# Sixteen wide matmuls, then sixteen narrow ones, and four buffers instead of three for the split weights

## The chip, the cores and the metric

The kernel runs on one core of a Trainium2 chip. Its time is the device time in microseconds (us) of one execution; the number that counts is the median of the runs. Five engines work side by side, each through its own list of instructions in order: TensorE (PE, with its weight loads PEld), VectorE (DVE), ScalarE (ACT), GpSimd (POOL, idle here) and SyncE (SP, which issues the DMAs).

## The reference

One decoder layer on a sequence of 256 tokens with 2048 features, in float32:

```python
h = rmsnorm(x, norm1_g) * (1 + sc1) + sh1              # sh, sc, g: columns of silu(c) @ w_ada
q_sb, k_sb, v_sb, q_ds, k_ds, v_ds, q_ix, k_ix, w_ix = split(h @ w_in)
o_sb = stick_breaking_attention(q_sb, k_sb, v_sb)       # 8 heads of 128
o_ds = dsa_attention(q_ds, k_ds, v_ds, q_ix, k_ix, w_ix)
x = x + g1 * (concat(rmsnorm(o_sb), rmsnorm(o_ds)) @ w_out)
h2 = rmsnorm(x, norm2_g) * (1 + sc2) + sh2
u = causal_conv3(h2 @ w_up);  gate, val = split(u)      # 2 x 5504 columns
x = x + g2 * ((silu(gate) * val) @ w_down)
return rmsnorm(x, final_norm_g)
```

## The kernel before

**Arithmetic.** The large products take float32 operands in two parts: a high part rounded to the matmul's 32-bit format and a low part that holds the rest. Each product is three products: high by high, high by low and low by high. `load` brings 1 MB of weights (128 x 2048) into one of four buffers called raw; a `wa` load, with the weights of the modulation vector, shares these four. `split` cuts a load into two halves of 1024 columns: ACT casts a half into a high tile `wh` (L145), and DVE subtracts it to get the low tile `wl` (L146). High and low tiles each rotate through three buffers, so ACT can cast a half only when PE has finished with the half three before it.

**Stages.** The program goes through the input projections (A, B, V, QK), the sparse attention, the eight stick-breaking heads, the output projection O, and the FFN (U is w_up, W is w_down). Up to the first eight column tiles of U, `trn` or `nat` issue three matmuls for each block of 128 features: in `trn`, L166 (high by high), L167 (high weights by the low part of the activations) and L168 (low weights), each with 256 columns. From the ninth column tile of U on, and in all of W, `fold` treats a half load of eight blocks: eight matmuls of 512 columns, in which the high weights meet the high and the low activations side by side (L160), then eight of 256 columns with the low weights (L162). There are 70 such loads in U and 43 in W, 113 in all, each with 32 matmuls.

**Heads.** One head (`sb_head`) is a chain between engines: three lines of PE make z (L664 to L666); ACT goes over it four times (L668 to L672); DVE ends the softplus (L673); PE makes u from it (L675, L676); DVE adds (L678), ACT takes exp (L679), PE makes o (L681, L682); ACT scales and squares it (L683, L688), and DVE adds the squares up (L689). Weights of the QK and O stages lie between these lines on all engines. In the same stretch PE makes four columns of the modulation vector (L195), which ACT copies to `rw` (L200) and PE transposes into `aq` (L203).

**Norms.** The rows of squares go through `rms_b`: PE sums them (`rsbp`, L115), ACT takes ln and exp (L119, L123), DVE sharpens the result in four small steps (L121 to L126), PE spreads it over the partitions (`rsbb`, L129) and ACT copies it out (L132). For the heads, `norm_o` then multiplies the heads by it (L647), ACT casts them to `osh` (L649) and DVE subtracts to get `osl` (L650). The second half of the rows of `w_out` (tiles `wO`m`1`) is multiplied with these two; the first half (`wO`m`0`) meets `odh` and `odl`, which come from the sparse attention earlier. The norm ahead of the FFN has the same form (`r2p`, `r2b`), followed by L305 to L307, which make the FFN's input.

**Order.** The Python text doesn't fix the order of work between independent steps. The framework's scheduler lays out each engine's list when the program is built; it takes the readiness of operands and the free buffers as it models them and otherwise keeps the order of the text. On the chip an engine follows its list as it stands.

Of the kernel before, what the change touches and what calls it, by code (L numbers as in the profile page):

```python
# [11 lines left out]
F32R = mybir.dt.float32r  # L12
BF16 = mybir.dt.bfloat16
I32 = mybir.dt.int32
AF = mybir.ActivationFunctionType
ALU = mybir.AluOpType
# [3 lines left out]
P = 128  # L20
# [18 lines left out]
PB, PN1, PN2, PSG, PDG, PCW, PCB, PC, PGF = 0, 96, 112, 128, 136, 144, 402, 488, 504  # L39
# [15 lines left out]
def layer(ctx: ExitStack, tc: tile.TileContext, a, out):  # L55
    nc = tc.nc
    V, A, T, DMA = nc.vector, nc.scalar, nc.tensor, nc.sync

    cp = ctx.enter_context(tc.tile_pool(name="cp", bufs=1))
    wp = ctx.enter_context(tc.tile_pool(name="wp", bufs=1))  # L60

    def b8(shape, dt, name):
        return wp.tile(shape, dt, name=name, tag="b8", bufs=17)

    def s2(shape, dt, name):
        return wp.tile(shape, dt, name=name, tag="s2", bufs=3)
# [6 lines left out]
    def ps(name, dt=F32, tag="ps"):  # L73
        pool, bufs = psum_pool[0]
        return pool.tile([P, 512], dt, name=name, tag=tag, bufs=bufs[tag])


    par = cp.tile([P, PW], F32, name="par")
# [23 lines left out]
    mod = cp.tile([P, 96], F32, name="mod")  # L102
# [3 lines left out]
    def rb(name):  # L106
        return wp.tile([P, S], F32, name=name, tag="rb", bufs=2)
# [27 lines left out]
    def load(src, n, name):  # L135
        w = wp.tile([P, 2048], F32, name=name, tag="raw", bufs=4)
        DMA.dma_start(out=w[:, 0:n], in_=src)
        return w
# [1 line left out]
    lo_ = [None, None]  # L140

    def split(w, off, n, name):
        wh = wp.tile([P, 1024], F32R, name=name + "h", tag="wh", bufs=3)
        wl = wp.tile([P, 1024], F32R, name=name + "l", tag="wl", bufs=3)
        lo_[1] = A.copy(out=wh[:, 0:n], in_=w[:, off:off + n])  # L145
        lo_[0] = V.tensor_tensor(out=wl[:, 0:n], in0=w[:, off:off + n], in1=wh[:, 0:n].bitcast(F32), op=ALU.subtract)  # L146
        return wh, wl

    def nat(pt, xh, xl, wh, wl, first, last):
# [2 lines left out]
        T.matmul(pt, lhsT=xh, rhs=wl, start=False, stop=False)  # L152
        T.matmul(pt, lhsT=xl, rhs=wh, start=False, stop=last)

    def fold(steps):

        for pt, x, wh, _, first, _ in steps:
            T.matmul(pt, lhsT=wh, rhs=x, start=first, stop=False)  # L160
        for pt, x, _, wl, _, last in steps:
            T.matmul(pt[:, 1, :], lhsT=wl, rhs=x[:, 0, :], start=False, stop=last)  # L162

    def trn(pt, xh, xl, wh, wl, first, last):

        T.matmul(pt, lhsT=wh, rhs=xh, start=first, stop=False)  # L166
        T.matmul(pt, lhsT=wh, rhs=xl, start=False, stop=False)  # L167
        T.matmul(pt, lhsT=wl, rhs=xh, start=False, stop=last)  # L168
# [14 lines left out]
    for i in range(1, 4):  # L183
        V.tensor_tensor(out=sq1[0][:, 0:4, :], in0=sq1[0][:, 0:4, :],
                        in1=sq1[i // 2][:, (i % 2) * 4:(i % 2) * 4 + 4, :], op=ALU.add)
# [25 lines left out]
    def order(later, earlier):  # L211
        tc.add_manual_dep(later.ins, earlier.ins.name,
                          mybir.DependencyInfo(mybir.DependencyClass.NoSync, mybir.DependencyReason.DATA),
                          reason="order")
# [57 lines left out]
    for g in range(4):  # L272
        pt = ps(f"cb{g}")
        for j in range(4):
            k = 4 * g + j
# [7 lines left out]
                           op1=ALU.mult)  # L283
    b1 = cp.tile([P, KT], F32, name="b1")
    V.scalar_tensor_tensor(out=b1, in0=par[:, PB + 16:PB + 32], scalar=1.0, in1=par[:, PN1:PN1 + KT], op0=ALU.add,
                           op1=ALU.mult)
# [228 lines left out]
    pt = ps("kixp", tag="att")  # L515
# [8 lines left out]
    for t in range(NT):  # L524
        for g in range(2):
            pt = ps(f"qixp{t}{g}", tag="att")
# [12 lines left out]
    for t in range(NT):  # L539
# [4 lines left out]
        for g in range(8 // npb):  # L544
            pts = [ps(f"rel{t}{g}{par_}", tag="att") for par_ in range(2)]
            for j in range(npb):
                for par_ in range(2):
                    T.matmul(pts[par_][:, j * L:(j + 1) * L],  # L548
                             lhsT=qixT[par_ * ID:(par_ + 1) * ID, g * npb + j, t * P:(t + 1) * P],
                             rhs=kixT[par_ * ID:(par_ + 1) * ID, 0:L], start=True, stop=True)  # L550
            for par_ in range(2):
                rl = s2([P, npb, L], F32, f"rl{t}{g}{par_}")
                A.activation(rl, pts[par_].rearrange("p (n l) -> p n l", n=npb), AF.Relu)  # L553
                for j in range(npb):
                    h = (g * npb + j) * 2 + par_
                    if sacc[par_] is None:
                        sacc[par_] = sc_t(L, f"sacc{t}{par_}")
                        if par_ == 0:
                            V.scalar_tensor_tensor(out=sacc[0], in0=rl[:, j, :], scalar=wix[:, t, h:h + 1], in1=cmt,
                                                   op0=ALU.mult, op1=ALU.add)  # L560
                        else:
                            V.tensor_scalar(out=sacc[1], in0=rl[:, j, :], scalar1=wix[:, t, h:h + 1], scalar2=None,
                                            op0=ALU.mult)
                    else:
                        V.scalar_tensor_tensor(out=sacc[par_], in0=rl[:, j, :], scalar=wix[:, t, h:h + 1],  # L565
                                               in1=sacc[par_], op0=ALU.mult, op1=ALU.add)
# [15 lines left out]
    pt = ps("kdsp", tag="att")  # L582
# [4 lines left out]
    for t in range(NT):  # L587
        for g in range(2):
            pt = ps(f"qdsp{t}{g}", tag="att")
# [6 lines left out]
    for t in range(NT):  # L596
# [4 lines left out]
        for g in range(NH // npb):  # L601
            pt = ps(f"lg{t}{g}", tag="att")
            pv = pt.rearrange("p (n l) -> p n l", n=npb)
            T.matmul(pv, lhsT=identb, rhs=mb[t].rearrange("p (n l) -> p n l", n=1).to_broadcast([P, npb, L]),
                     start=True, stop=False)
            for j in range(npb):
                T.matmul(pv[:, j, :], lhsT=qdsT[:, g * npb + j, t * P:(t + 1) * P], rhs=kdsT[:, 0:L],
                         start=False, stop=j == npb - 1)
# [8 lines left out]
            for j in range(npb):  # L617
                h = g * npb + j
                A.activation(pr[:, h, :], pr[:, h, :], AF.Copy, scale=rec[:, j:j + 1])
        for s_ in range(t + 1):  # L620
            for g in range(2):
                pt = ps(f"pp{t}{s_}{g}", tag="att")
# [3 lines left out]
        for g in range(2):  # L626
            pt = ps(f"av{t}{g}", tag="att")
            pv = pt.rearrange("p (k t) -> p k t", k=4)
            for s_ in range(t + 1):
                T.matmul(pv, lhsT=a2[:, s_, 80 + HD:80 + 2 * HD], rhs=pT[:, s_, 4 * g:4 * g + 4, :],  # L630
                         start=s_ == 0, stop=s_ == t)
            A.activation(dsq[:, 4 * g:4 * g + 4, t * P:(t + 1) * P], pv, AF.Square)
            for j in range(4):
                h = 4 * g + j
# [76 lines left out]
    acc = [ps(f"O{m}", tag="acc") for m in range(4)]  # L711
# [11 lines left out]
    resid_i, last = [None, None], [None, None]  # L723
    x1T = [b8([P, 8, S], F32, f"x1T{i}") for i in range(2)]
    sq2 = ws[:, 1536:1792]

    def resid(dst, acc, gate, res, sqsum, k, name):

        resid_i[0] = V.scalar_tensor_tensor(out=dst, in0=acc, scalar=gate, in1=res, op0=ALU.mult, op1=ALU.add)  # L729
        if k == 0:  # L730
            A.activation(sqsum, dst, AF.Square)
            return None
        sq = s2([P, S], F32, f"{name}{k}")
        resid_i[1] = A.activation(sq, dst, AF.Square)  # L734
        if k >= KT - 2:
            return sq
        V.tensor_tensor(out=sqsum, in0=sqsum, in1=sq, op=ALU.add)

    for m in range(8):
# [6 lines left out]
        for p_ in range(2):  # L746
            k = 2 * m + p_
# [36 lines left out]
    def bank(name):  # L784
        return pool3.tile([P, 2, S], F32, name=name, tag="ps", bufs=8)
# [6 lines left out]
    def do_U(f, i):  # L792

        if i == 0:
            uacc[f] = [bank(f"U{f}{gv}") for gv in range(2)] if f >= G0 else bank(f"U{f}")
        w = load(a["wU"][f, i], 2048, f"wU{f}{i}")
        for gv in range(2):
            wh, wl = split(w, gv * 1024, 1024, f"wU{f}{i}{gv}")
            if (f, i, gv) in ((0, 0, 1), (1, 0, 0)):
                order(lo_[0], resid_i[0])  # L800
                if gv == 0:
                    order(lo_[1], resid_i[1])
            steps = []
            for j in range(8):
                k = 8 * i + j
                x = h2[k // 4][:, k % 4, :, :]
                sl = slice(j * P, (j + 1) * P)
                if f >= G0:
                    steps.append((uacc[f][gv], x, wh[:, sl], wl[:, sl], k == 0, k == KT - 1))
                else:  # L810
                    trn(uacc[f][:, gv, :], x[:, 0, :], x[:, 1, :], wh[:, sl], wl[:, sl], k == 0 and gv == 0,
                        k == KT - 1 and gv == 1)
            fold(steps)

    def eager(n=2):
        for k in range(KT):
# [4 lines left out]
    for f in range(G0):  # L821
        do_U(f, 0)
        pump()
        if f >= 3:
            eager()
    for k in range(8, KT):
        h2_make(k)
    for f in range(FT):
# [3 lines left out]
        acc = uacc.pop(f)  # L832
# [9 lines left out]
        for gv in range(2):  # L842
# [3 lines left out]
            for sft in (1, 2):  # L846
                o = PCW + 3 * i + 2 - sft
                V.scalar_tensor_tensor(out=uc[:, gv, sft:S], in0=u[:, gv, 0:S - sft], scalar=par[:, o:o + 1],  # L848
                                       in1=uc[:, gv, sft:S], op0=ALU.mult, op1=ALU.add)
# [12 lines left out]
    sq3, last = rb("sq3"), [None, None]  # L862
    wacc = {}
    for q in range(FT):
        w = load(a["wD"][:, q * 2048:(q + 1) * 2048], 2048, f"wD{q}")
        for p_ in range(2):
            wh, wl = split(w, p_ * 1024, 1024, f"wD{q}{p_}")
            steps, done = [], None
            for j in range(8):
                k, f = divmod((2 * q + p_) * 8 + j, FT)  # L870
                if f == 0:
                    wacc[k] = bank(f"W{k}")
                steps.append((wacc[k], aT[f // 4][:, f % 4, :, :], wh[:, j * P:(j + 1) * P], wl[:, j * P:(j + 1) * P],
                              f == 0, f == FT - 1))
                if f == FT - 1:
                    done = k
            fold(steps)
            if done is not None:
                k = done
                acc = wacc.pop(k)  # L880
                xk = x1T[k // 8][:, k % 8, :]
                g = mod[:, 80 + k:81 + k]
                V.scalar_tensor_tensor(out=xk, in0=acc[:, 0, :], scalar=g, in1=xk, op0=ALU.mult, op1=ALU.add)  # L883
                last[k % 2] = resid(xk, acc[:, 1, :], g, xk, sq3, k, "x2q")
                A.activation(xk, xk, AF.Copy, scale=par[:, PGF + k:PGF + k + 1])
    r3 = rms_b([sq3] + last, D, None, "r3", "ps")
    for k, n in ((0, 2), (2, 2), (4, 4), (8, 4), (12, 4)):
        y = x1T[k // 8][:, k % 8:k % 8 + n, :]
# [72 lines left out]
```

## Time and profile before

| | |
|---|---|
| median of 3 runs | 1207.88 us (1207.71 to 1208.54) |
| profiled execution, its own time | 1209.0 us |
| its span, first to last instruction | 1207.2 us |
| PE busy | 1154.3 us, 96% of the span |
| DVE busy | 886.8 us, 73% |
| ACT busy | 630.6 us, 52% |
| mean granted TensorE clock | 0.982 of full speed |
| stretch of `fold`, first to last matmul | 562.36 to 1193.54 us |

Busy time says how long an engine worked. What a change is worth is read from what PE waits for, stage by stage. The median lies 1.1 us below the profiled execution's own time, and 1.8 us of that time lie outside the span.

### The profile page before, as it was taken

The page shows a single profiled execution, that of the slowest core. Times are in us where ns is not written, and L with a number is a line of the kernel's source. Part 1 is how long each engine was busy: PE and PEld are TensorE (multiplying, and loading weights), DVE is VectorE, ACT ScalarE, POOL GpSimd, SP SyncE. Part 2 cuts the span into 40 slices and gives each one's busy share as a digit, 9 for nine tenths or more (in the row PEclk, how much of TensorE's full clock was granted, in tenths as well). Part 3 has the DMA queues.
Part 4 walks back from the last instruction along what each step waited for, and adds up shares of the span by engine and source line. Part 5 has one row for each costly group of instructions (what it writes and reads, how often), then busy time and mean ns, then how long its engine had stood idle before and what let it go on. Part 6 is the DMA issues. An engine that isn't in the chain of part 4 may idle for free.

```text
span 1207.2 us, 17866 instructions
## 1 busy us (share of the span) xinstructions
PE 1154.3 (96%) x7120; PEld 1015.3 (84%) x7120; DVE 886.8 (73%) x1267; ACT 630.6 (52%) x1004; POOL 0.2 (0%) x4
## 2 busy tenths in 40 slices
PE   3699999899999998999999999999999999999996
PEld 2478997668879998999888888888888888888885
DVE  4876788699868888878799878787787645555553
ACT  3356554448566445466555555555555544444441
POOL 0000000000000000000000000000000000000000
PEclk9799999899999998999999999999999999999998
DMA  8988999758788896865578657566565555545531
GB/s 309 375 328 311 333 333 353 283 192 326 284 298 331 287 358 247 325 247 212 198 276 300 241 207 266 205 232 237 210 227 191 188 197 179 200 180 189 195 140 69
DMA packets 43282, 303.48 MB, mean 251 GB/s; under 512 B 4928, under 2 KB 5440, under 8 KB 7232
## 3 DMA queue, kind: packets, MB, share of 16 engines
q1 hardware_dynamic: 43200, 302.35, 68.3%
q8 instruction: 55, 0.90, 0.3%
q14 instruction: 27, 0.22, 0.0%
HBM read 300.24 MB, written 2.10 MB: 250 GB/s over the span
## 4 chain that ended last, share of the span: by engine, by line
PE 88%; DVE 5%; ACT 3%; DMA 2%; issue 1%; SPq 0%; DVEq 0%; ACTq 0%
PE U L160 21%; PE W L160 13%; PE U L162 11%; PE W L162 7%; PE U L166 3%; PE U L167 3%; PE U L168 3%; PE O L166 3%; PE O L168 3%; PE O L167 3%; PE QK L166 2%; PE QK L167 2%; PE QK L168 2%; DVE wa L218 2%; PE ap L195 1%
## 5 line engine op out<-in xcount | busy, mean ns | idle before, releaser
L218 DVE SCALAR_TENSOR_TENSOR wa<-wa,scb 128x2048 f32<-128x2048 f32 x76 | 173.4, 2284 | 5.3 <-DMA wa<-wa 5.2
L848 DVE SCALAR_TENSOR_TENSOR uc<-u,par,uc 128x255 f32<-128x255 f32 (+1 forms) x140 | 66.4, 480 | 17.6 <-ACT uc L844 15.7
L844 ACT ACTIVATE uc<-u,par 128x256 f32<-128x256 f32 x70 | 42.0, 600 | 40.3 <-DVE u L838 40.3
L838 DVE TENSOR_TENSOR u<-U,u 128x256 f32<-128x256 f32 x70 | 29.2, 417 | 0.7 <-ACT u L837 0.7
L316 ACT ACTIVATE amul<-mod,b,par 128x1 f32<-128x1 f32 x32 | 12.0, 385 | 29.2 <-DVE wa L218 29.2
L837 ACT COPY u<-U 128x256 f32<-128x256 f32 x70 | 25.3, 362 | 0.0
L195 PE MATMUL ap<-wg,csil 128*32 128x512 f32 x160 | 23.4, 640 | 0.6 <-DMA wg<-wg 0.3
L883 DVE SCALAR_TENSOR_TENSOR x1T<-W,mod,x1T 128x256 f32<-128x256 f32 x16 | 7.7, 484 | 21.9 <-PE W L162 21.9
L319 ACT ACTIVATE mod<-mod,par 128x1 f32<-128x1 f32 x32 | 8.7, 294 | 24.0 <-DVE wa L218 23.1
L855 ACT CAST aT<-uc 128x256 fp32r<-128x256 f32 x43 | 17.4, 404 | 3.1 <-DVE uc L854 3.1
L854 DVE TENSOR_TENSOR uc<-uc 128x256 f32<-128x256 f32 x43 | 18.1, 421 | 1.0
L850 ACT ACTIVATE uc<-uc 128x256 f32<-128x256 f32 x43 | 17.8, 415 | 0.4 <-DVE uc L848 0.4
L856 DVE TENSOR_TENSOR aT<-uc,aT 128x256 fp32r<-128x256 f32 x43 | 18.0, 418 | 0.0
L848 DVE SCALAR_TENSOR_TENSOR uc<-U,par,uc 128x255 f32<-128x255 f32 (+1 forms) x32 | 15.2, 478 | 1.1 <-ACT uc L844 0.6
L734 ACT ACTIVATE x2q<-x1T 128x256 f32<-128x256 f32 x15 | 6.2, 416 | 14.6 <-DVE x1T L729 14.4
L195 PEld LDWEIGHTS ap<-wg,csil 128*32 128x32 f32 x160 | 4.3, 114 | 9.2 <-issue 6.9
L548 PE MATMUL rel<-ws,qixT 64*128 64x128 f32 (+1 forms) x64 | 9.9, 392 | 1.5 <-ACT rl L553 1.5
L276 PE MATMUL cb<-ident,csil 128*128 128x128 f32 x16 | 3.6, 423 | 7.6 <-DMA ident<-ident 7.6
L151 PE MATMUL A<-wA00h,hh 128*128 128x512 f32 x4 | 2.5, 669 | 8.5 <-ACT hh L311 8.5
L565 DVE SCALAR_TENSOR_TENSOR scw<-rl,wix,scw 128x128 f32<-128x128 f32 (+1 forms) x28 | 10.4, 408 | 0.0
L679 ACT ACTIVATE sbt<-sbt 128x384 f32<-128x384 f32 x8 | 4.2, 526 | 11.8 <-DVE sbt L678 11.8
L729 DVE SCALAR_TENSOR_TENSOR x1T<-O,mod,xT 128x256 f32<-128x256 f32 x16 | 7.0, 478 | 4.2 <-PE O L168 4.2
(2810 smaller groups left out, 4030.4 us busy)
## 6 DMA issues: line engine op xcount, KB each, us to landing
wU<-wU SPq DMA_DIRECT2D x86, 1024.0 KB, 4.8
wa<-wa SPq DMA_DIRECT2D x76, 1024.0 KB, 6.2
wD<-wD SPq DMA_DIRECT2D x43, 1024.0 KB, 4.6
wg<-wg SPq DMA_DIRECT2D x20, 1024.0 KB, 6.9
wA<-wA SPq DMA_DIRECT2D x16, 1024.0 KB, 7.2
wQK<-wQK SPq DMA_DIRECT2D x16, 1024.0 KB, 7.2
wO<-wO SPq DMA_DIRECT2D x16, 1024.0 KB, 6.5
xT<-xT SPq DMA_DIRECT2D x4, 512.0 KB, 6.0
```

The lines of the kernel that those rows point to most:

```text
L160: T.matmul(pt, lhsT=wh, rhs=x, start=first, stop=False)
L162: T.matmul(pt[:, 1, :], lhsT=wl, rhs=x[:, 0, :], start=False, stop=last)
L166: T.matmul(pt, lhsT=wh, rhs=xh, start=first, stop=False)
L167: T.matmul(pt, lhsT=wh, rhs=xl, start=False, stop=False)
L168: T.matmul(pt, lhsT=wl, rhs=xh, start=False, stop=last)
L195: T.matmul(pt[32 * j:32 * j + 32, :], lhsT=csil[:, k:k + 1].to_broadcast([P, 32]), rhs=w[:, j * 512:(j + 1) * 512], start=q == 0, stop=q == 3)
L218: i = V.scalar_tensor_tensor(out=w, in0=w, scalar=1.0, in1=scb, op0=ALU.mult, op1=ALU.mult, accum_out=mod[:, j:j + 1])
L837: A.copy(out=u[:, gv, :], in_=acc[gv][:, 1, :])
L838: V.tensor_tensor(out=u[:, gv, :], in0=acc[gv][:, 0, :], in1=u[:, gv, :], op=ALU.add)
L844: A.activation(uc[:, gv, :], u[:, gv, :], AF.Identity, scale=par[:, PCW + 3 * i + 2:PCW + 3 * i + 3], bias=par[:, PCB + i:PCB + i + 1])
L848: V.scalar_tensor_tensor(out=uc[:, gv, sft:S], in0=u[:, gv, 0:S - sft], scalar=par[:, o:o + 1], in1=uc[:, gv, sft:S], op0=ALU.mult, op1=AL ...
L854: V.tensor_tensor(out=uc[:, 1, :], in0=uc[:, 0, :], in1=uc[:, 1, :], op=ALU.mult)
```

## The change

`fold` is called once for a load instead of once for a half: sixteen matmuls of 512 columns stand in a row, then sixteen of 256. A flag remembers which kind ended the load ahead; when that was the 256-column kind and no accumulation begins in this load, the 256-column ones go first. High and low tiles get four buffers each. In W, the work on a finished feature block follows the whole load instead of its half.

```diff
-        wh = wp.tile([P, 1024], F32R, name=name + "h", tag="wh", bufs=3)
-        wl = wp.tile([P, 1024], F32R, name=name + "l", tag="wl", bufs=3)
+        wh = wp.tile([P, 1024], F32R, name=name + "h", tag="wh", bufs=4)
+        wl = wp.tile([P, 1024], F32R, name=name + "l", tag="wl", bufs=4)
...
+    narrow = [False]
     def fold(steps):
-        for pt, x, wh, _, first, _ in steps:
-            T.matmul(pt, lhsT=wh, rhs=x, start=first, stop=False)
-        for pt, x, _, wl, _, last in steps:
-            T.matmul(pt[:, 1, :], lhsT=wl, rhs=x[:, 0, :], start=False, stop=last)
+        lo_first = narrow[0] and not any(s[4] for s in steps)
+        for lo in (lo_first, not lo_first):
+            for pt, x, wh, wl, first, last in steps:
+                stop = last and lo != lo_first
+                if lo:
+                    T.matmul(pt[:, 1, :], lhsT=wl, rhs=x[:, 0, :], start=False, stop=stop)
+                else:
+                    T.matmul(pt, lhsT=wh, rhs=x, start=first, stop=stop)
+        narrow[0] = not lo_first
...
     # do_U
+        steps = []
         for gv in range(2):
...
-            steps = []
...
-            fold(steps)
+        fold(steps)
...
     # W
+        steps, done = [], None
         for p_ in range(2):
...
-            steps, done = [], None
...
-            fold(steps)
-            if done is not None:
+        fold(steps)
+        if done is not None:
```

The new lines move later line numbers by 7: L166 to L168 are L173 to L175 in the rows of the change, L218 is L225, L305 is L312, L647 is L654, L650 is L657. The scheduler also lays out other lists for the engines, in all stages that split weights. Three places follow.

**The norm of the heads, on PE.** Rows of PE's list of before around `rsbp` and `rsbb`; `O_3204` to `O_3207` are the accumulators of the first four pairs of feature blocks:

```order
L195 MATMUL ap_3184<-wg_3266,csil 32x512 x4
L115 MATMUL rsbp<-nones,ws 128x1 x2
L203 MATMUL aq_3274<-ident,rw_3272 128x128 x4
L166 MATMUL O_3205<-odh,wO100h 128x256
...
L167 MATMUL O_3206<-odl,wO200h 128x256
L129 MATMUL rsbb<-ident,rsby 128x128 x2
L168 MATMUL O_3206<-odh,wO200l 128x256
...
L168 MATMUL O_3207<-odh,wO301l 128x256
L166 MATMUL O_3204<-osh,wO010h 128x256
```

And of the change, at the same work:

```order
L175 MATMUL O_3207<-odh,wO301l 128x256
L115 MATMUL rsbp<-nones,ws 128x1 x2
L129 MATMUL rsbb<-ident,rsby 128x128 x2
L173 MATMUL O_3204<-osh,wO010h 128x256
L173 MATMUL O_3205<-osh,wO110h 128x256
L174 MATMUL O_3204<-osl,wO010h 128x256
L175 MATMUL O_3204<-osh,wO010l 128x256
```

Before, 50 matmuls stood between `rsbp` and `rsbb`, and 94 between `rsbb` and the first one that needs `osh`. Now none stands at either place, and `rsbp` comes after all the work that doesn't need it.

On DVE, rows of the change around the same norm (`wa_3678` is a load of the modulation weights):

```order
L146 TENSOR_TENSOR wO110l<-wO_3554,wO110h 128x1024
L146 TENSOR_TENSOR wO111l<-wO_3554,wO111h 128x1024
L121 TENSOR_SCALAR rsbv<-rsbp 128x2
L225 SCALAR_TENSOR_TENSOR wa_3678,mod<-wa_3678,scb 128x2048
L124 SCALAR_TENSOR_TENSOR rsbl<-rsby 128x2
L125 TENSOR_TENSOR rsbl<-rsbl,rsbv 128x2
L126 SCALAR_TENSOR_TENSOR rsby<-rsbl,rsby 128x2
L654 TENSOR_TENSOR os<-os,rsb 128x1024 x2
L657 TENSOR_TENSOR osl<-os,osh 128x1024 x2
```

Before, the row ahead of `rsbv` was the sum for `aq`, and the splits of `wO110` and `wO111` came behind the two `osl` rows. A `wa` row stood between L121 and L124 then too. On ACT, the cast of `wO111h` now stands right ahead of the ln of this norm.

**The norm ahead of the FFN, on DVE.** Rows of before, then of the change (`wU_4414` is the second load of U, `g_0` the first row of the FFN's input):

```order
L146 TENSOR_TENSOR wU100l<-wU_4414,wU100h 128x1024
L121 TENSOR_SCALAR r2v<-r2p 128x2
L124 SCALAR_TENSOR_TENSOR r2l<-r2y 128x2
L125 TENSOR_TENSOR r2l<-r2l,r2v 128x2
L126 SCALAR_TENSOR_TENSOR r2y<-r2l,r2y 128x2
L305 SCALAR_TENSOR_TENSOR g_0_4304<-x1T_3485,amul,r2b 128x256
```

```order
L146 TENSOR_TENSOR wU100l<-wU_4414,wU100h 128x1024
L121 TENSOR_SCALAR r2v<-r2p 128x2
L146 TENSOR_TENSOR wU101l<-wU_4414,wU101h 128x1024
L124 SCALAR_TENSOR_TENSOR r2l<-r2y 128x2
L125 TENSOR_TENSOR r2l<-r2l,r2v 128x2
L126 SCALAR_TENSOR_TENSOR r2y<-r2l,r2y 128x2
L225 SCALAR_TENSOR_TENSOR wa_4531,mod<-wa_4531,scb 128x2048
L312 SCALAR_TENSOR_TENSOR g_0_4304<-x1T_3485,amul,r2b 128x256
```

Two rows have moved into the chain: the split of `wU101`, and a `wa` row. On ACT, the cast of `wU101h` now stands between the ln and the exp of this norm.

**The sixth and the eighth head.** Rows of PE's list of the change at the sixth head (`u_2999`, `o_3004`):

```order
L682 MATMUL u_2999<-sbt,cst 128x384
L683 MATMUL u_2999<-sbt,nones 128x128
L173 MATMUL O_3204<-odh,wO000h 128x256
L174 MATMUL O_3204<-odl,wO000h 128x256
L175 MATMUL O_3204<-odh,wO000l 128x256
L688 MATMUL o_3004<-sbt,vsb 128x256
```

Before, eleven QK matmuls, whose weights had long been split, stood between this head's u and o. On DVE, the subtraction that makes `wO000l` comes right behind this head's L685 (L678 of before). ACT's list of the change at the eighth head (`z_3158`) is the following; `rw_3272` is the copy for which the `aq` rows on PE wait:

```order
L675 COPY sbt<-z_3158 128x384
L677 ACTIVATE sbt<-z_3158 128x384
L678 ACTIVATE sbt<-sbt 128x384
L323 ACTIVATE amul<-mod,b_191,par 128x1
L679 ACTIVATE sbt<-sbt 128x384
L207 COPY rw_3272<-ap_3184 128x512
```

On PE the `aq` rows now stand between this head's z and u, behind four O rows and the last four `ap` rows. Before, the copy to `rw` came after the last head, and the `aq` rows after `rsbp`.

## Rows read from the trace of the kernel before

**Rows 1.** The page: shares of the chain that ended last, by engine.

```profile
PE 88%; DVE 5%; ACT 3%; DMA 2%; issue 1%; SPq 0%; DVEq 0%; ACTq 0%
```

**Rows 2.** Windows: stretch, length, busy PE, PEld, DVE, ACT, POOL, clock, DMA share, GB/s.

```profile
562.36:1193.54 631.18, 631.18 (x3618) 555.45 (x3617) 434.25 (x587) 327.60 (x470) 0.00 (x0) 1.00 0.58 207
```

**Rows 3.** Timeline of PE, start of `fold`: start, length, engine, line, count.

```profile
562.36 2.00 PE L160 MATMUL U<-h,wU800h 128*128 128x512 f32 x8
564.20 1.12 PE L162 MATMUL U<-h,wU800l 128*128 128x256 f32 x8
565.15 2.00 PE L160 MATMUL U<-h,wU801h 128*128 128x512 f32 x8
```

**Rows 4.** Timeline of PE, V: two of 22 matmuls in a row.

```profile
101.22 0.39 PE L151 MATMUL V<-V0000h,hh 128*128 128x512 f32 x1
...
105.98 0.39 PE L151 MATMUL V<-V0040h,hh 128*128 128x512 f32 x1
```

**Rows 5.** Timeline of PE, QK: two of 102 matmuls in a row.

```profile
149.77 0.28 PE L167 MATMUL QK<-hl,wQK0410h 128*128 128x256 f32 x1
...
161.89 0.28 PE L166 MATMUL QK<-hh,wQK0610h 128*128 128x256 f32 x1
```

**Rows 6.** Timeline of PE, second head's o: idle time and releaser in brackets.

```profile
323.77 0.70 PE L681 MATMUL o<-sbt,vsb 128*128 128x256 f32 x2 [0.29 <-ACT sbt L679]
```

**Rows 7.** Timeline of the eighth head, all engines.

```profile
363.97 0.33 PE L664 MATMUL z<-sbm,identb 128*128 128x384 bf16 x1
...
364.70 0.36 PE L168 MATMUL O<-odh,wO000l 128*128 128x256 f32 x1
...
366.44 0.53 ACT L672 ACTIVATE sbt<-sbt 128x384 f32<-128x384 f32 x1
...
367.62 0.91 PE L675 MATMUL u<-sbt,cst 128*128 128x384 f32 x2
...
368.79 0.56 DVE L678 TENSOR_TENSOR sbt<-u,sbt 128x384 f32<-128x384 f32 x1 [1.23 <-PE u L676]
```

**Rows 8.** Timeline of the norm of the heads, all engines.

```profile
372.20 1.07 PE L195 MATMUL ap<-wg,csil 128*32 128x512 f32 x8
...
373.19 0.61 PE L115 MATMUL rsbp<-nones,ws 128*128 128x1 f32 x4
373.33 0.58 ACT L200 COPY rw<-ap 128x512 f32<-128x512 f32 x1 [1.46 <-PE ap L195]
373.84 0.26 ACT L119 ACTIVATE rsbl<-rsbp,epsc 128x2 f32<-128x2 f32 x1
...
374.82 2.28 DVE L218 SCALAR_TENSOR_TENSOR wa<-wa,scb 128x2048 f32<-128x2048 f32 x1
```

**Rows 9.** Timeline of ACT and DVE, from `rsbb` to `osl`.

```profile
380.86 0.37 ACT L132 COPY rsb<-rsbb 128x256 f32<-128x256 f32 x1 [1.45 <-PE rsbb L129]
...
381.27 1.22 DVE L647 TENSOR_TENSOR os<-os,rsb 128x1024 f32<-128x1024 f32 x1 [0.41 <-ACT rsb L132]
...
382.53 1.05 ACT L649 CAST osh<-os 128x1024 fp32r<-128x1024 f32 x1 [0.34 <-DVE os L647]
...
386.29 1.05 ACT L145 CAST wO010h<-wO 128x1024 fp32r<-128x1024 f32 x1 [0.45 <-PE O L167]
```

**Rows 10.** Timeline of the norm ahead of the FFN.

```profile
463.78 0.26 ACT L119 ACTIVATE r2l<-r2p,epsc 128x2 f32<-128x2 f32 x1 [0.21 <-PE r2p L115]
...
464.81 0.15 DVE L124 SCALAR_TENSOR_TENSOR r2l<-r2y 128x2 f32<-128x2 f32 x1
...
465.19 0.16 DVE L126 SCALAR_TENSOR_TENSOR r2y<-r2l,r2y 128x2 f32<-128x2 f32 x1
...
466.28 1.26 DVE L305 SCALAR_TENSOR_TENSOR g<-x1T,amul,r2b 128x256 f32<-128x256 f32 x3 [0.93 <-ACT r L132]
```

**Rows 11.** Windows of the norm ahead of the FFN and of the start of U.

```profile
461.20:467.60 6.40, 2.00 (x15) 1.50 (x13) 5.00 (x12) 3.41 (x8) 0.00 (x0) 0.91 0.94 369
467.60:473.30 5.70, 5.61 (x26) 5.64 (x27) 5.70 (x12) 2.72 (x7) 0.00 (x0) 0.50 0.00 0
```

More of the change, by code (lines that the diff above doesn't have):

```diff
@@ L876, in layer @@
                     done = k
-            fold(steps)
-            if done is not None:
[L879 to L885, printed above, removed]
+        fold(steps)
+        if done is not None:
+            k = done
+            acc = wacc.pop(k)
+            xk = x1T[k // 8][:, k % 8, :]
+            g = mod[:, 80 + k:81 + k]
+            V.scalar_tensor_tensor(out=xk, in0=acc[:, 0, :], scalar=g, in1=xk, op0=ALU.mult, op1=ALU.add)
+            last[k % 2] = resid(xk, acc[:, 1, :], g, xk, sq3, k, "x2q")
+            A.activation(xk, xk, AF.Copy, scale=par[:, PGF + k:PGF + k + 1])
     r3 = rms_b([sq3] + last, D, None, "r3", "ps")
```

## Prediction, made blind

> **What bounds the kernel.** I began with the chain that ended last: PE has 88% of it [rows 1], so the time is PE's list plus what PE waits for. Next the windows of the stretch in which `fold` runs: 631.18 us at full clock, PE busy in all of it, while DVE has 434 us and ACT 328 [rows 2]. PE waits for nobody there, so the edit of `fold` can only win what PE itself loses between two matmuls. Outside that stretch I read PE's timeline for idle time. PE takes its list as it stands: at the second head's o it stood idle for 0.29 us until the exp was done, though QK matmuls with split weights stood behind the blocked row [rows 6]. So where the changed lists put a row whose operand is late, PE waits, and work that has moved elsewhere doesn't fill the gap.
>
> **What the long runs bring.** A half load takes 2.79 us (565.15 - 562.36), of which the eight wide matmuls take 1.84 and the eight narrow ones 0.95 [rows 3]; over the stretch it is 631.18 / 226 = 2.793 [rows 2]. In a long run a wide matmul comes every (105.98 - 101.22) / 21 = 0.2267 us [rows 4], a narrow one every (161.89 - 149.77) / 101 = 0.120 [rows 5]. Eight of each at these spacings are 2.774, so one turn to narrow and back costs 0.0195 us. Before, there are 226 such pairs. Now the kind changes once within a load and mostly not between loads: 35 pairs for the 70 loads of U, and in W, where a load in which a block begins must start wide, some 27. The 164 pairs that go are worth 164 x 0.0195 = **3.2 us**. Bounds: nothing (if the cost lies with the start of a new block of weights rather than with the turn), and 226 x 0.0195 = 4.4.
>
> A rule of the Trainium skill gives more. "TensorE: Matmul & The Clock Gate", section "Back-to-back issue gap", gives 216 ns for a warm 512-column matmul and 109 ns for one of 256 columns; by these figures eight of each are 2.600 us, the whole excess of 0.193 per group would be the turns', and the gain an estimated 31.7 us. The runs of 22 and of 102 matmuls here show 227 and 120 ns at granted clock 1.00, without a turn, so the trace disagrees.
>
> In a load that begins narrow, PE needs the low tiles first. Such a load's two casts (1.05 us each) and subtractions (1.22 each, as a DVE row of that size [rows 9]) take about 3.4 us in a chain, and PE works 5.55 us on the load ahead; with four buffers the first half of the next load can be split while that one runs. I cost this at **0**; a rival below holds the other case.
>
> **The norm of the heads.** Before, 144 matmuls lay between `rsbp` and the first use of `osh`, 17 us of cover. Now there are none, and `rsbp` comes after all work that needs only `odh`. Let T be the end of O_3207's last odh matmul. Behind it: ACT casts `wO111h`, for which it waits until PE leaves a high tile, as it did for `wO010h` before [rows 9]: ready at T + 1.2. DVE subtracts `wO111l` until T + 2.4; only then `rsbv`; the `wa` row takes 2.28 [rows 8], until T + 4.7; L124 to L126 take 0.54 (464.81 to 465.35) and the spread with its copy 0.93 [rows 10], so L647 starts at T + 6.2. It ends 1.26 later (the cast followed at 382.53 after 381.27), the cast takes 1.05 and the first `osl` 1.22 [rows 9]: T + 9.7. PE has only two rows with `osh` and the small ones of the norm to fill it, 0.9 us with what starts late: a wait of 8.8, and with a late landing of the `wa` load up to 0.5 more; I take **9.0**. Bounds: 0 and 9.5. The `osh` row alone ends at T + 8.5, so nearly all of it stands before the first of these rows, a wait right behind `rsbb`.
>
> PE's clock. After the norm ahead of the FFN, where PE was busy for 2.00 of 6.40 us, the granted clock was 0.50 (1.2 GHz) for 5.7 us: 26 matmuls of 256 columns instead of the 47 that fit at 0.120 [rows 11]. The new wait is longer than that one, so I add the loss of such a stretch: 5.7 - 26 x 0.12 = 2.6, taken as **2.4**. Bounds: 0 and 2.6. "TensorE: Matmul & The Clock Gate", section "Why this matters for your kernels", of the Trainium skill advises against idle gaps of PE between bursts of matmuls, since it then falls to half clock; these rows agree, and without it the sum would be 2.4 lower.
>
> **The norm ahead of the FFN.** The cast of `wU101h` now stands between ln and exp, and its subtraction (1.22) in front of L124. Ln starts at 463.78 [rows 10]; the cast ends about 1.3 later, the subtraction at about 466.3, so L124 is late by 466.3 - 464.81 = 1.5. The `wa` row of 2.28 then stands between L126 and the first g, where before 0.93 passed while PE and ACT spread the result [rows 10]: 1.35 more. Sum 2.85, taken as **2.8**; bounds 1.5 (if that load has landed so late that the row would be hidden) and 2.9. The half clock behind it was there before [rows 11] and is not counted again.
>
> **The heads.** From z to u a head needs 367.62 - 364.70 = 2.92 us of other rows on PE [rows 7]. At the eighth head these were O rows. Now PE has `aq` rows there, which need the copy to `rw`, and this comes last on ACT: from z's start to L672 2.47, then a one-column row (about 0.3, nearest row the ln's 0.26), 0.53 and 0.58: 3.9 [rows 7, 8]. PE is there after 0.73 for z, four O rows at 0.12 and four `ap` rows (372.20 to 373.19) 0.99: 2.2 [rows 7, 8]. A wait of 1.7. At the sixth head the third O row needs `wO000l`, whose subtraction stands behind L678: 1.17 after u's start, 0.47 (a head's row of 0.56 less its overlap), 1.22: 2.9, where PE comes at about 1.15 [rows 7]: 1.75. Elsewhere among the heads the changed list leaves some 24 QK rows (2.88) or a dozen `ap` rows in a gap that needs 2.92; I count 1.5 for them. Less the waits of before that fall away, of which the 0.29 of [rows 6] is one, some 0.9 in all: **4.1**. Bounds: 1 (each late row finds its operand there but the two above by half) and 7 (none of the old waits falls away and the small ones are twice as long). The norm of the sparse attention moves ahead of its squares' last sum a little: **0.4**, from 0 to 0.8.
>
> **The sum.** 1209.0 (the profiled execution's own time) - 3.2 + 9.0 + 2.4 + 2.8 + 4.1 + 0.4 = 1224.5. The median of the runs is 1.1 below the profiled time, so the forecast is **1223.4 us**, slower by 1.3%.
>
> **Rivals.**
>
> *The heads' waits are covered and the clock holds.* Speaks for it: the late rows were worked out from gaps of one head, and a wait at one row gives the rows behind it slack. Against: the waits at o were there before [rows 6], and the clock fell after every idle stretch like this that I looked at, as in [rows 11]. Time: 1223.4 - 4.1 - 2.4 = 1216.9.
>
> *Each load that begins narrow waits for a subtraction.* 51 loads begin so. If the low half is split only after the load ahead has left its tiles, each pays 1.22: 62 us, 1286. It decides if a subtraction ends later than the last row of the load ahead. Against: DVE has 434 of 631 us [rows 2], and with four high and low tiles half a load is ahead.
>
> *The waits cost nothing (faster).* The place is the norm of the heads: if `osh` were ready when PE comes to it, and so at the other two places, only the long runs are left: 1207.9 - 3.2 = 1204.7. It decides when the waits together are under 3.2. Against: nothing stands in PE's list between `rsbp` and the `osh` rows, and ACT and DVE alone need the 6.2 us to L647 and 2.3 more for the cast [rows 9, 10].
>
> *Long runs are faster than those of V and QK.* A row would have to gain 15.5 us / 3616 = 4.3 ns to break even; at 10 ns the time is 1223.4 - 36 = 1187. Against: 22 and 102 matmuls without a turn keep the spacing of [rows 4, 5]. This is also where the rule on the issue gap would lead.
>
> **How the numbers follow.** The main case has 0.76, its own range 1217 to 1229 (the heads by -3 and +3, the clock by -2.4, the norm by -1 and +0.5, the runs by +3.2). The first rival has 0.12, the loads that wait 0.04, no waits 0.06, faster runs 0.02. The range 1214 to 1230 takes in the main case and the first rival. About 0.2%, 2.4 us, is what a measurement of this kernel can tell from no change. Faster: 0.08 from the last two rivals; within 0.2%: 0.02, part of the main case's far end; slower: 0.90.
>
> **What would show it.** Right: PE in `fold` with 32 rows at 0.2267 and 0.120 and one small step; an idle stretch of about 9 us before the first rows with `osh`, and granted clock 0.50 behind it; the first g 2.8 us later after `r2p` than before; waits of 1.7 at the last `aq` rows and at the sixth head's third O row. Wrong: spacings in `fold` that differ from the short runs' by more than 3 ns, waits of PE in U or W, or an `osh` that is ready when PE comes.

## The result, and the profile after

The changed kernel takes 1220.66 us (median of 5 runs, 1219.15 to 1222.48) where the kernel before takes 1207.9: a ratio of 1.0102, with a 95% interval of 1.0089 to 1.0116. (The ratios in this document are estimates of their own, each with its interval, and can differ by some 0.1% from the quotient of two medians.) The forecast was 1223.4 us, with a range of 1214 to 1230. The profiled execution's own time is 1222.48 us and its span 1220.7, against 1209.0 and 1207.2 before. It is the slowest of the five, so stages are compared between the two profiled executions, and their 13.5 us stand against 12.8 between the medians.

The page of the change, shares of the chain that ended last:

```profile
PE 89%; DVE 6%; ACT 3%; DMA 1%; issue 1%; SPq 0%; DVEq 0%; ACTq 0%
```

Against [rows 1], DVE has one point more of the chain, and so has PE; the shares alone don't say where. The waits of PE from the heads to the start of U say where (what waits, for what; us in all, times, longest):

```profile
PE rsbb L129 <- DVE rsby L126: 4.7, 1, 4.7
PE r2b L129 <- DVE r2y L126: 3.1, 1, 3.1
PE O L173 <- ACT osh L656: 2.8, 1, 2.8
PE U L173 <- DVE g L312: 2.7, 1, 2.7
PE O L175 <- DVE wO000l L146: 1.5, 1, 1.5
PE aq L210 <- ACT rw L207: 1.2, 1, 1.2
...
PE QK L175 <- DVE wQK1600l L146: 0.6, 1, 0.6
PE O L174 <- DVE osl L657: 0.5, 1, 0.5
```

Before, `rsbb`, `osh`, `osl` and `wO000l` weren't in the list, and at the norm ahead of the FFN it had:

```profile
PE U L166 <- ACT h L306: 1.9, 1, 1.9
PE r2b L129 <- DVE r2y L126: 1.7, 1, 1.7
```

The norm of the heads, timeline of all engines:

```profile
394.50 0.50 PE L115 MATMUL rsbp<-nones,ws 128*128 128x1 f32 x4
394.64 1.04 ACT L145 CAST wO111h<-wO 128x1024 fp32r<-128x1024 f32 x1 [1.84 <-PE O L174]
395.59 0.26 ACT L119 ACTIVATE rsbl<-rsbp,epsc 128x2 f32<-128x2 f32 x1
395.72 1.23 DVE L146 TENSOR_TENSOR wO111l<-wO,wO111h 128x1024 fp32r<-128x1024 f32 x1 [1.67 <-ACT wO111h L145]
...
396.93 2.28 DVE L225 SCALAR_TENSOR_TENSOR wa<-wa,scb 128x2048 f32<-128x2048 f32 x1
...
399.52 0.16 DVE L126 SCALAR_TENSOR_TENSOR rsby<-rsbl,rsby 128x2 f32<-128x2 f32 x1
...
399.74 0.69 PE L129 MATMUL rsbb<-ident,rsby 128*128 128x128 f32 x2 [4.73 <-DVE rsby L126]
...
400.87 2.36 DVE L654 TENSOR_TENSOR os<-os,rsb 128x1024 f32<-128x1024 f32 x2 [1.19 <-ACT rsb L132]
402.12 2.18 ACT L656 CAST osh<-os 128x1024 fp32r<-128x1024 f32 x2 [1.29 <-DVE os L654]
...
403.22 0.58 PE L173 MATMUL O<-osh,wO010h 128*128 128x256 f32 x1 [2.80 <-ACT osh L656]
```

T of the prediction is 394.50, where `rsbp` starts right behind the last row with `odh`. The subtraction of `wO111l` and the `wa` row stand between `rsbp` and the small steps, as the order list has them; L126 ends at T + 5.2, the first `os` row starts at T + 6.4 (forecast 6.2), the first `osh` row at T + 8.7 (8.5).

The norm ahead of the FFN, timeline of all engines:

```profile
477.93 0.26 ACT L119 ACTIVATE r2l<-r2p,epsc 128x2 f32<-128x2 f32 x1 [0.21 <-PE r2p L115]
478.09 1.03 ACT L145 CAST wU101h<-wU 128x1024 fp32r<-128x1024 f32 x1
...
479.15 1.23 DVE L146 TENSOR_TENSOR wU101l<-wU,wU101h 128x1024 fp32r<-128x1024 f32 x1
480.30 0.15 DVE L124 SCALAR_TENSOR_TENSOR r2l<-r2y 128x2 f32<-128x2 f32 x1
...
480.76 2.28 DVE L225 SCALAR_TENSOR_TENSOR wa<-wa,scb 128x2048 f32<-128x2048 f32 x1
...
482.97 1.26 DVE L312 SCALAR_TENSOR_TENSOR g<-x1T,amul,r2b 128x256 f32<-128x256 f32 x3
```

From ln to the first g it is 5.04 us; in [rows 10] it is 2.50. The subtraction and the `wa` row fill the difference.

Windows of the change: the stretch of `fold`, then three pieces behind the norm of the heads.

```profile
579.24:1207.14 627.90, 627.90 (x3618) 556.06 (x3617) 426.37 (x586) 331.40 (x469) 0.00 (x0) 1.00 0.59 207
...
399.70:404.86 5.16, 1.86 (x5) 1.17 (x6) 3.99 (x4) 2.46 (x3) 0.00 (x0) 0.50 0.75 313
404.86:408.28 3.42, 3.42 (x18) 3.42 (x18) 0.70 (x1) 0.00 (x0) 0.00 (x0) 0.50 0.00 0
408.28:410.00 1.72, 1.72 (x15) 1.72 (x15) 0.00 (x0) 0.84 (x1) 0.00 (x0) 0.95 0.00 0
```

The stretch of `fold` has become 631.18 - 627.90 = 3.28 us shorter [rows 2], with PE busy all the time. Behind the norm the clock stands at 0.50 (1.2 GHz) while PE waits and for another 3.4 us of dense rows. The long runs, timeline of PE in W:

```profile
984.88 1.12 PE L166 MATMUL W<-aT,wD30l 128*128 128x256 f32 x8
985.84 1.12 PE L166 MATMUL W<-aT,wD31l 128*128 128x256 f32 x8
986.80 2.00 PE L168 MATMUL W<-aT,wD30h 128*128 128x512 f32 x8
988.64 1.98 PE L168 MATMUL W<-aT,wD31h 128*128 128x512 f32 x8
990.46 1.98 PE L168 MATMUL W<-aT,wD40h 128*128 128x512 f32 x8
992.27 1.98 PE L168 MATMUL W<-aT,wD41h 128*128 128x512 f32 x8
```

Eight narrow rows take 0.96. The first eight wide rows behind a turn take 1.84, the next eight 1.82 and then 1.81: a turn slows only the first rows behind it, and wide rows still come every 0.227 us far from one.

### The profile page after: what moved, and what is told of

It reads as the page before. It is cut to its first block, busy times and chain, and to the rows that moved or that the text cites. A ratio compares the mean times of both kernels' runs of the same rounds, so it can differ in the third digit from the quotient of the medians.

```text
span 1220.7 us, 17725 instructions
## 1 busy us (share of the span) xinstructions
PE 1154.4 (95%) x7120; PEld 1018.6 (83%) x7120; DVE 879.5 (72%) x1267; ACT 632.2 (52%) x1004; POOL 0.2 (0%) x4
## 4 chain that ended last, share of the span: by engine, by line
PE 89%; DVE 6%; ACT 3%; DMA 1%; issue 1%; SPq 0%; DVEq 0%; ACTq 0%
PE U L168 21%; PE W L168 13%; PE U L166 11%; PE W L166 7%; PE U L173 3%; PE U L174 3%; PE U L175 3%; PE O L174 3%; PE O L175 3%; PE QK L173 3%; PE QK L175 3%; PE O L173 3%; PE QK L174 3%; DVE wa L225 2%; PE ap L202 1%; PE A L151 1%
## 5 line engine op out<-in xcount | busy, mean ns | idle before, releaser
L225 DVE SCALAR_TENSOR_TENSOR wa<-wa,scb 128x2048 f32<-128x2048 f32 x76 | 173.2, 2284 | 3.8 <-DMA wa<-wa 3.5
L855 DVE SCALAR_TENSOR_TENSOR uc<-u,par,uc 128x255 f32<-128x255 f32 (+1 forms) x140 | 63.8, 478 | 0.8
L207 ACT COPY rw<-ap 128x512 f32<-128x512 f32 x5 | 2.9, 581 | 15.5 <-PE ap L202 15.5
```

What stands on the lines that cost most here:

```text
L225: i = V.scalar_tensor_tensor(out=w, in0=w, scalar=1.0, in1=scb, op0=ALU.mult, op1=ALU.mult, accum_out=mod[:, j:j + 1])
```

## The experiments

Two theories stood against each other. *Lists*: the turns in `fold` pay 3.2 us, and all of the loss comes from what the fourth buffer does to the engines' lists ahead of U. *Shape*: `fold` over a whole load, or additional buffers as such, cost the time. The kernel before, run beside the experiments, had medians of 1208.6 to 1208.7 us.

**The new fold with three buffers of each kind**

```diff
-        wh = wp.tile([P, 1024], F32R, name=name + "h", tag="wh", bufs=4)
-        wl = wp.tile([P, 1024], F32R, name=name + "l", tag="wl", bufs=4)
+        wh = wp.tile([P, 1024], F32R, name=name + "h", tag="wh", bufs=3)
+        wl = wp.tile([P, 1024], F32R, name=name + "l", tag="wl", bufs=3)
```

> The new fold with three high and three low buffers, as before the change. The lists of all engines up to the ninth column tile of U are those of before; in the stretch of fold 68 wide runs stand instead of 226. Theory (the lists cost, the turns pay): 158 turn pairs less at 0.0195 us, so 1207.9 - 3.1 = 1204.8 us, stretch of fold 628.1 us, norm of the heads and heads as before. Rival (a whole load at a time needs the fourth buffer: a load that begins narrow waits for a subtraction): PE waits in U and W, from about 0.5 us at some 45 loads (1227) up to 1.22 at each. Second rival (the new shape of fold is what made the change slow): 1217 or more.

Measured: 1206.69 us, ratio 0.9984 (0.9974 to 0.9994). Windows of the stretch of `fold`, and the one wait of PE in it:

```profile
560.52:1189.89 629.37, 628.75 (x3618) 556.00 (x3617) 430.13 (x587) 331.48 (x470) 0.00 (x0) 1.00 0.59 208
```

```profile
PE U L166 <- DVE wU1601l L146: 0.6, 1, 0.6
```

The stretch gains 1.8 us instead of 3.1. By the starts of its rows PE loses some 1.4 us here, and 1.1 of it at `wU160` and the load behind it, which both begin wide: DVE comes late to one subtraction, having worked without a break since 645.75, through two `wa` rows among others. The second of them, and that subtraction:

```profile
648.30 2.29 DVE L225 SCALAR_TENSOR_TENSOR wa<-wa,scb 128x2048 f32<-128x2048 f32 x1
...
653.89 1.22 DVE L146 TENSOR_TENSOR wU1601l<-wU,wU1601h 128x1024 fp32r<-128x1024 f32 x1
```

Loads that begin narrow lose 0.1 to 0.2 us at three places, 0.3 to 0.4 in all, and not 0.5 or 1.22 at each. The shape of `fold` is not what made the change slow.

**Four buffers with the old fold** (the two lines above with `bufs=4` in the kernel before)

> Four high and four low buffers with the old fold. The lists up to the ninth column tile of U are those of the change, 226 wide runs as before. Theory: all of the loss and none of the gain: 1220.7 + 3.2 = 1223.9 us, with the wait of 4.7 and 2.8 us around rsbb, 1.7 and 1.8 at the heads, and the first g 2.6 us late. Rival (four buffers take waits away and fold is what costs): 1208 or less.

Measured: 1223.66 us, ratio 1.0131 (1.0117 to 1.0144). The waits are those of the change (4.7 for `rsbb`, 3.1 for `r2b`, 2.8 for `osh`, 2.7 for the first g, 1.5 for `wO000l`, 1.2 for `rw`), and the stretch of `fold` is 631.18 us, as before. Its window, and the largest wait:

```profile
576.93:1208.11 631.18, 631.18 (x3618) 555.45 (x3617) 432.47 (x586) 326.81 (x469) 0.00 (x0) 1.00 0.59 206
```

```profile
PE rsbb L129 <- DVE rsby L126: 4.7, 1, 4.7
```

The buffers alone bring the loss, and more of it than the whole change.

**Three high buffers, four low ones** (the change with `bufs=3` for `wh`)

> The whole change, but with three high buffers and four low ones. The lists up to the ninth column tile of U are those of before; 63 wide runs. Theory (it is the fourth high buffer that lays out the stages before U anew): 1207.9 - 163 x 0.0195 = 1204.7 us. Rival (any additional buffer costs, whichever it is): 1214 to 1221.

Measured: 1205.3 us, ratio 0.9974 (0.9962 to 0.9986), the lowest median of all kernels here and faster than before. Ahead of U the lists of PE, ACT and DVE are those of before, row for row, and nothing new stands in the list of waits there. Window of the stretch of `fold`, 2.8 us shorter than before:

```profile
562.99:1191.39 628.40, 628.27 (x3618) 556.02 (x3617) 426.69 (x587) 335.17 (x470) 0.00 (x0) 1.00 0.60 208
```

The additional low buffer costs nothing.

**Four high buffers, three low ones** (the change with `bufs=3` for `wl`)

> The whole change, but with four high buffers and three low ones. PE's list differs from that of the change in 33 rows of the stretch of fold and nowhere else; 72 wide runs instead of 62. Theory (the fourth high buffer alone lays the stages before U out anew): 1220.7 + 10 x 0.0195 = 1220.9 us, with the same waits around rsbb, at the heads and at the first g. Rival (it takes both additional buffers): 1205 to 1210.

Measured: 1225.22 us, ratio 1.0134 (1.011 to 1.0158), 4.3 us above the forecast, a miss. The high buffer alone gives PE the list of the change ahead of U, and the waits at `wO000l` and `rw` are 1.5 and 1.2 again. But ACT's and DVE's lists there are neither those of before nor those of the change, and both norms cost less. At the norm of the heads the `wa` row now stands behind the small steps, and PE waits 1.7 and 4.0 us at `rsbb` and `osh` instead of 4.7 and 2.8:

```profile
393.76 1.23 DVE L146 TENSOR_TENSOR wO110l<-wO,wO110h 128x1024 fp32r<-128x1024 f32 x1 [1.65 <-PE O L175]
...
395.51 0.16 DVE L126 SCALAR_TENSOR_TENSOR rsby<-rsbl,rsby 128x2 f32<-128x2 f32 x1
395.59 2.28 DVE L225 SCALAR_TENSOR_TENSOR wa<-wa,scb 128x2048 f32<-128x2048 f32 x1
```

At the norm ahead of the FFN neither the split of `wU101` nor a `wa` row stands in the chain, and the first row of U comes 1.0 us later after `r2p` than before instead of 2.5. The loss is in U, where PE now waits. Waits of PE in the stretch of `fold`:

```profile
PE U L166 <- DVE wU3711l L146: 1.0, 1, 1.0
PE U L166 <- DVE wU2711l L146: 0.9, 1, 0.9
PE U L166 <- DVE wU1711l L146: 0.9, 1, 0.9
```

The stretch is 633.9 us long, 6 more than in the change. By the starts of the rows ten loads pay, 0.2 to 1.3 us each, and all ten begin narrow. So the two fourth buffers do different work: the high one moves the lists, and next to it loads that begin narrow need the fourth low one.

**Half loads that begin with the kind that ended the half ahead** (three buffers; `fold` as in the change, called for a half as before)

> Three buffers, fold for a half load as before, but a half begins with the kind that ended the half ahead where no accumulation begins: 154 wide runs, while the weights still change 226 times, half by half. Theory (the cost is the turn): 72 pairs x 0.0195 = 1.4 us less, 1206.5, and a stretch of fold of 629.8. Rival (the cost is the change to a new half block of weights): 1207.9, stretch 631.2.

Measured: 1206.7 us, ratio 0.9993 (0.9984 to 1.0002), which can't be told from no change. The trace can tell; window of the stretch of `fold`:

```profile
562.94:1192.69 629.75, 629.75 (x3618) 555.74 (x3617) 436.42 (x587) 331.86 (x470) 0.00 (x0) 1.00 0.59 207
```

72 turn pairs less made it 631.18 - 629.75 = 1.43 us shorter, 0.0199 for a pair, with as many changes of weights as before. It is the turn that costs.

**The norm of the heads written earlier**

```diff
-    for m in range(4):
+    for m in range(2):
         do_O(acc[m], m, 0, odh, odl)
         pump()
...
     norm_o(os_, rsb, osh, osl)
     pump()
+
+    for m in range(2, 4):
+        do_O(acc[m], m, 0, odh, odl)
+        pump()
```

> The whole change, with the norm of the heads (rms_b and norm_o) written between the second and the third call of do_O. PE's list is that of the change up to rsbp, which now comes before the O rows of the third and fourth pair: 24 rows stand between rsbp and rsbb, 74 between rsbb and the first osh row. Theory (the wait of 9.1 us around rsbb and the 1.6 us at half clock behind it come from rsbp's place in the list): both go, 1220.7 - 10.7 = 1210.0 us, 0.2% above before; the waits at the heads and the late first g stay. Rival (the operands of the norm are late in the four-buffer lists wherever rsbp stands): 1218 or more.

Measured: 1210.58 us, ratio 1.0019 (1.001 to 1.0028). `rsbb`, `osh` and `osl` are gone from the list of waits; the others stay at 3.1, 2.7, 1.5 and 1.2. In the trace 22 rows stand between `rsbp` and `rsbb`, and 72 between `rsbb` and the first `osh` row (24 and 74 were expected). Four buffers and all, the norm costs nothing once its first row has rows behind it.

**Rows that keep PE busy during the wait** (the change with 36 additional matmuls behind `rsbp` and 22 behind `rsbb`)

```diff
+    def warm(n, prev):
...
+        pt = ps(f"dm{n}", tag="att")
+        for _ in range(n):
+            i = T.matmul(pt[:, 0:S], lhsT=odh[:, 0, 0:P], rhs=odh[:, 0, :], start=True, stop=True)
+            order(i, prev)
+            prev = i
+        return prev
...
+            tail[0] = warm(36, m)
...
+            tail[0] = warm(22, m)
```

Further orderings keep `rsbp` behind the last row with `odh`, and the first `osh` row behind the 22.

> The whole change, with 36 matmuls of 256 columns between rsbp and rsbb and 22 between rsbb and the first osh row, whose result nobody reads (additional work, no wait taken away). Theory (the clock falls because PE stands idle): granted clock 1.00 in the rows behind the norm, the first full-rate row 1.6 us earlier after the osh operands are there, 1219.1 us; in the trace the osh rows come as late after rsbp as before, some 8.5 us. Rival (the lower clock comes with the O rows or with ACT and DVE, not with PE's idle time): still 0.50 for some 3 us, 1220.7. Second rival (the additional rows delay the norm): 1221 or more.

Measured: 1218.57 us, ratio 1.0086 (1.0072 to 1.0099). Windows from `rsbb` on:

```profile
399.70:405.00 5.30, 4.37 (x35) 3.96 (x34) 4.70 (x4) 2.32 (x3) 0.00 (x0) 1.00 0.62 252
405.00:408.00 3.00, 3.00 (x28) 3.00 (x27) 0.42 (x1) 1.05 (x1) 0.00 (x0) 1.00 0.00 0
```

The first `osh` row comes 8.5 us after `rsbp`, about as late as in the change, and the clock stays at 1.00. From that row to the fifth pair's first `osh` row it is 29.91 us (402.31 to 432.22) instead of 31.66 (403.22 to 434.88), while ACT's and DVE's lists ahead of U are those of the change. The half clock is a matter of PE's idle time, and it cost 1.7 us.

**Both norms mended** (the early norm, and the split of `wU101` ordered behind the norm's steps)

```diff
+            if (f, i, gv) == (1, 0, 1):
+                order(lo_[0], after[0])
+                order(lo_[1], ex_[0])
```

> As the run with the early norm, and the cast and subtraction of the second load's second half of U are ordered behind the exp and the last small step of the norm ahead of the FFN; the modulation row ahead of the first g stays. Theory: of the 2.7 us at that norm the 1.5 of the subtraction go, 1208.5 us, about the time of before; first g about 3.7 us after r2p instead of 5.2. Rival (the first g waits for the modulation row alone, which starts when its load is there): 1210.

Measured: 1207.78 us, ratio 0.9994 (0.9985 to 1.0003). From ln, from which the 3.7 and 5.2 of the expectation count, to the first g it is 3.71 us (467.66 - 463.95). The `wa` row still keeps 1.2 of the difference to before. The median is 2.8 us below that of the run with the early norm, and 1.3 of that show at this norm; in the two profiled executions another 1.5 lie in the sparse attention, ahead of any change between the two lists. With 3.2 us at the heads against 3.3 won in `fold`, a time near that of before is what is to be expected.

**The late norm in the kernel before** (`m` is a row of `rsbp`, `tail` the last O row with `odh`)

```diff
+                if name == "rsb":
+                    order(m, tail[0])
```

> The kernel before, three buffers and the old fold, with one thing added: rsbp is ordered behind the last O row that doesn't need osh. Theory (the place of rsbp alone makes the wait): L126 about 1.7 us after rsbp, the first os row 0.93 later, the first osh ready at 4.9, then a modulation row of 2.28 ahead of osl, which is ready at 8.4; PE waits for some 7.5 us and has half clock for some 3 us behind that, so 9 us slower than before, 1217 us. Rival (with three buffers the norm's operands come early, and the place costs nothing): 1208.

Measured: 1220.36 us, ratio 1.0104 (1.009 to 1.0118), 3 us more than expected. Timeline of PE from `rsbb` on (lines are 2 later in this run, so L128 is L126 of before):

```profile
395.54 0.43 PE L131 MATMUL rsbb<-ident,rsby 128*128 128x128 f32 x2 [2.50 <-DVE rsby L128]
...
398.77 0.58 PE L170 MATMUL O<-osh,wO010h 128*128 128x256 f32 x1 [2.80 <-ACT osh L653]
...
402.18 0.58 PE L171 MATMUL O<-osl,wO010h 128*128 128x256 f32 x1 [2.61 <-DVE osl L654]
```

One ordering costs the kernel before as much as the whole change. I had left out the split of `wO110`, which stands ahead of L123 here, 1.2 us; and the clock stayed at 0.50 for longer, until 408.1, 5.9 us from the first `osl` row on. The way the wait is made stands; both sizes were too small.

## Why the prediction was right

The sum was 1224.5 us against a profiled time of 1222.48, some 2 us too much: the terms for the clock, the heads and the norm of the sparse attention were too large. (The bounds of the main case add up to 1230.1 at the upper end, and not to 1229.) By its own terms:

- **Long runs**, forecast -3.2, measured -3.28, with 62 turn pairs left as counted. The half-load run puts a pair at 0.0199 and the bound "nothing" aside. The figures of the Trainium skill ("TensorE: Matmul & The Clock Gate", section "Back-to-back issue gap"), which that section gives for a matmul by itself and by which the gain would have been an estimated 31.7, don't hold for these rows: the third group of eight wide rows in a run still takes 1.81 us, 0.227 for a row.
- **Waits of narrow-led loads**, forecast 0, measured 0: PE is busy in all of 627.90 us. With four high buffers this takes the fourth low one: with three low ones the loads that begin narrow lost 6 us. With three of each they lost only 0.3 to 0.4.
- **Norm of the heads**, forecast 9.0; PE's waits at `rsbb`, `osh` and `osl`, taken as the excess of its row starts over the usual spacing, are 4.9, 3.0 and 1.0 with what lies between them, 9.1 in all. One claim was off: I expected nearly all of it in front of the `osh` row. That row waits as I said, but 4.7 of the time stands before `rsbb` already.
- **Clock**, forecast 2.4, measured 1.6 to 1.7, the first mis-sized term. I took the loss of a stretch in which dense rows fill all 5.7 us [rows 11]. Here 0.50 began during the wait (the clock is 1.00 from 394.50 to 398.20 and 0.50 from 398.30 on), where it costs nearly nothing, and only 3.42 us of dense rows were left at it. In the run of the late norm it was 5.9 us. That idle time is the cause is shown; what sets the length was not tried.
- **Norm ahead of the FFN**, forecast 2.8; the first g is 2.54 later after ln, and the first row of U too (6.45 instead of 3.92). The half clock behind it, which I had not counted again, cost 0.2 more than before.
- **Heads**, forecast 4.1, measured some 3, the second mis-sized term. The two waits I walked through came out (`aq`: forecast 1.7, measured 1.8; `wO000l`: 1.75 and 1.7, both as the delay of the row's start). The 1.5 for small ones was 0.9, 0.7 of it at `wQK1600l`, and the old waits that fell away were 1.2 and not 0.9. This term is uneven: with the same lists ahead of U, the second head's wait for exp was 0.3 us before, and 1.3, 0.7 and 1.4 in the runs with three of each, with four low ones and with the half loads.
- **Norm of the sparse attention**, forecast 0.4: PE had no wait there, before or now. The whole stage of the sparse attention is 0.7 longer by its rows' spacing, in many small pieces. This stage also differs between executions of one list. Here is the same window of the change and of the run with four buffers and the old fold, whose lists up to there are the same:

```profile
215.00:300.00 85.00, 79.58 (x461) 59.71 (x460) 70.53 (x175) 49.41 (x122) 0.00 (x0) 0.94 0.71 264
215.00:300.00 85.00, 79.00 (x484) 59.86 (x481) 72.58 (x180) 50.26 (x123) 0.00 (x0) 1.00 0.75 277
```

  The granted clock is 0.94 in one and 1.00 in the other, and the stage is some 3 us longer in the first. The kernel before had 0.94 there in its profiled execution too, so the comparison above is fair; but 3 us between two single executions need not come from an edit.

Stage by stage, by the spacing of PE's rows, the change differs from before by -0.2 up to the sparse attention, 0.7 in it, 3.1 in the heads, 10.6 from `rsbp` to `r2p` (the norm of the heads with its clock), 2.5 to the first row of U, 0.2 to the start of `fold` and -3.3 in it. That is 13.6; the spans differ by 13.5. That the heads' part comes from QK rows which four buffers let run out earlier was argued from the lists; no run took it away alone.

## What to carry to other kernels

A buffer count is an input of whatever lays out the lists: look at what the lists do in every stage that shares the tag, also where the buffer isn't wanted. A reduction whose result gates later rows should be given a place in the list ahead of independent work, since work that has been used up in front of it can't hide it. A gain of about one ns for each of 3616 rows is soon lost to one chain that PE has to sit out; here the gain could be had without the loss by adding the low buffer alone.

## What the runs showed that I had not expected

The two fourth buffers act apart. With four high and three low ones PE waited in the stretch of `fold`, some 6 us that neither the change nor three of each had. And half clock after idle time cost 1.6 us in the change and 2.7 us behind the late norm (27 rows in 5.92 us, where 27 x 0.120 = 3.24 would do). In both the clock fell inside the wait: at 398.2 in the change, and in the run of the late norm between 397.8, up to which it is 1.00, and 398.0, from which it is 0.50. They differ in how long 0.50 went on over dense rows, 3.42 and 5.92 us.
